# One joined state product in DeltaNet's scan, and HGRN2's recurrence over 128 tokens in place of two chunks of 64

## The chip, the cores and the metric

The kernel runs as one program on one core of a Trainium2 chip. The metric is the device time of one execution in microseconds (us). Engines: PE is TensorE, DVE is VectorE, ACT is ScalarE, POOL is GpSimd, SP is SyncE, which issues nearly all DMAs. A change of 0.3% is about what a measurement of this kernel can tell from no change.

## The reference

Two layers of a hybrid decoder trunk over 1024 tokens with a model width of 1024, all float32. Each layer normalises its input, projects it, feeds three groups of heads (A: sliding-window attention, B: HGRN2, C: gated DeltaNet), projects their joined output back, and ends with a SwiGLU feed-forward part of width 2816. What the change concerns are B and C, four heads of 64 each:

```python
# B, HGRN2: per chunk of 64 tokens and per head
kt = -expm1(lf); cum = cumsum(lf, axis=2)
attn = einsum('bhtd,bhsd,bhtsd->bhts', qt, kt, decay)   # decay = exp(cum_t - cum_s), s <= t
o = attn @ vt + einsum('bhtd,bhde->bhte', qt * exp(cum), state)
state = exp(last) * state + einsum('bhsd,bhse->bhde', kt * exp(last - cum), vt)
...
# C, gated DeltaNet: per chunk of 64 tokens and per head
v_new = u - w @ state
o = qd @ state + qkc @ v_new
state = gl * state + swapaxes(kd, -1, -2) @ v_new
...
out = rmsnorm(o, gain) * silu(gate)      # both groups
```

The result of B doesn't depend on the size of its chunks: a longer chunk holds more of the sum in `attn` and less in `state`.

## The kernel before, in words

The tokens are handled in two halves of 512, the layers in turn, so there are four passes (layer, half): (0,0), (0,1), (1,0), (1,1). In each, dense products (input projection, output projection, feed-forward) run on PE as three float32r products per block (lines 776 to 778 in `mm3`: high by high, and the two cross terms of a high/low split of both operands). Their weights come by DMA into `wraw`, ACT rounds them to `whi` (line 747), DVE makes the rest `wlo` (line 748).

The three head groups, the mixers, are Python generators: `gdn` (DeltaNet), `hgrn` and `attention`. Each handles four blocks of 128 tokens per pass, so 16 blocks in all. Every `yield` ends a step; the class `Pace` asks a `Weaver` for the next step after so many dense products (`tick`), so that the steps are strewn among the dense work of another stage: the mixers of (0,0) among input projections, those of the other three passes among the feed-forward part of the pass before. That fixes the order in which instructions are written down. Their order on each engine is then made by the tile framework's scheduler, which also hands out buffers: pools have a number of buffers per tag, and a tile whose pool is full waits until an earlier one was read for the last time. `k.pb` (3 PSUM banks) serves HGRN2 and attention, `k.pc` (2 banks) DeltaNet, `k.mp` (one buffer per tag) the SBUF tiles of the mixers.

A PE matrix product has a shape of array: operands of 64 rows and 64 columns use a 64x64 tile of the 128x128 array, and the profile writes `64*64`, `128*64` or `128*128` for it. A plain float32 product shows as two records in the trace, a transpose or a float32r product as one.

- `hgrn`, one block: lines 430 to 447 transpose `kk` (432), make the sums of log forget gates for six halving levels plus one in `pd` (four tiles of 448 columns, 438) and their exponentials `E`, and the decayed keys `kd` (444 to 447). Lines 450 to 457 multiply `E` with keys and queries into `X` for the levels 32, 16, 8, 4, 2, 1: keys on POOL for odd places in the list, on DVE for even, queries on DVE. Lines 459 to 477: 64x64 products per level into `pl` (470), which DVE picks together into `st` under masks (474, 477). Lines 479 to 502, twice, once per chunk of 64: output from the state (484, operands of 64 columns), from `st` (488), the state's update (494) and four DVE instructions on 64x64 that put it into `sB` (500). `finish` follows.
- `gdn`, one block: lines 574 to 608 load and normalise; 610 to 623 transpose keys, queries, decayed queries `qd` and `kb` and copy them out (`qdT` is used by the scan); 633 to 638 are the 64x64 products `pkk`, of which 643 and 644 on DVE make `AT` and `qkT` from the tiles r = 0 and r = 1; then a triangular solve on DVE (654 to 669). Lines 694 to 722, twice, once per chunk: `w` by the state (701, 64 columns), new values `vn` on DVE (703), then decayed queries by the state (706, 64 columns), `qkT` by `vn` (709) and the state's update (715), and four DVE instructions (720).
- `finish` (376 to 396) squares the output of one block on ACT (384), multiplies by the gate on DVE (385), scales by a reciprocal root, transposes (392), and stores to `mix`. Its tile `f_sq` has the tag `f1`, one buffer for HGRN2 and DeltaNet.
- `build_consts` makes the masks and sums on POOL and DVE at the start (lines 89 to 124).

Of the kernel before, what the change touches and what calls it, by code (L numbers as in the profile page):

```python
# [29 lines left out]
LEVELS = [32, 16, 8, 4, 2, 1]  # L30
LN_FLOOR = 60
# [31 lines left out]
def build_consts(k, positions):  # L63
# [5 lines left out]
    mc = t1[:, 0:896].rearrange("p (l t) -> p l t", l=7)  # L69
    idt = t1[:, 896:1024]  # L70
# [26 lines left out]
    sel(mc[:, 6, :], [[1, 128]], 0, -1)  # L97
    G.memset(mc[0:64, 6, 64:128], 0.0)
    k.mc = cp.tile([128, 7, 128], F32R, name="mcr")
    V.tensor_copy(k.mc, mc)  # L100
    k.tri = k.mc[:, 6, :].bitcast(F32)
# [18 lines left out]
    k.cst = cp.tile([128, 128], F32R, name="cst")  # L120
    G.memset(mk, 1.0)
    sel(mk, [[-1, 128]], -1, 1)
    G.memset(mk[64:128, 0:64], 0.0)
# [252 lines left out]
def finish(k, mixr, po, gate, t0, b, pt, junk):  # L376
    nc = k.nc
    V, A, G, T = nc.vector, nc.scalar, nc.gpsimd, nc.tensor
    sp = k.mp
    p4 = po.rearrange("p (h d) -> p h d", d=64)  # L380
    sq = sp.tile([128, 4, 64], F32, name="f_sq", tag="f1")
    ss = k.small.tile([128, 4], F32, name="f_ss")
    for j in range(4):
        A.activation(junk[:, j, :], p4[:, j, :], AF.Square, accum_out=ss[:, j:j + 1])
    V.tensor_tensor(out=sq, in0=p4, in1=gate.rearrange("p (h d) -> p h d", d=64), op=ALU.mult)
    r = k.small.tile([128, 4], F32, name="f_r")
    rsqrt(k, r, ss, 4, 1.0 / 64, EPS)
    V.tensor_tensor(out=sq, in0=sq, in1=bc(r[:, :, None], (128, 4, 64)), op=ALU.mult)
    yield 6.0
    pt = pt()  # L390
    for p in range(2):
        T.transpose(pt[:, p, :], sq[:, 2 * p:2 * p + 2, :].rearrange("p a b -> p (a b)"), k.ident)
    ot = sp.tile([128, 4, 128], F32, name="f_ot", tag="fo")
    A.activation(ot[:, 0:2, :], pt, AF.Copy)
    nc.sync.dma_start(out=mixr[:, t0:t0 + 2, 128 * b:128 * b + 128], in_=ot[:, 0:2, :])
    yield 0.0


def hgrn(k, lc, l, h, src, r2):
# [4 lines left out]
    E = r2[:, 0:1792].rearrange("p (a l t) -> p a l t", a=2, l=7)  # L404
    X = r2[:, 1792:3328].rearrange("p (a l t) -> p a l t", a=2, l=6)
    kT = r2[:, 3328:3584].rearrange("p (a t) -> p a t", a=2)
    qd = r2[:, 3584:3840].rearrange("p (a t) -> p a t", a=2)
    st = r2[:, 3840:4096].rearrange("p (r a t) -> p r a t", r=2, a=2)
# [12 lines left out]
    for b in range(NB):  # L421
        nc.sync.dma_start(out=ld[:, 512:1024], in_=tmr[:, b, C_BV:C_BV + 512])
        qT = mp.tile([128, 2, 128], F32, name="h_qT")
# [10 lines left out]
        for p in range(2):  # L434
            for hf in range(2):
                pd = k.pb.tile([128, 448], F32, name="pd", tag="b")
                for i, t_ in enumerate((lfh, lfl)):
                    T.matmul(pd, t_[:, 128 * p:128 * p + 128], mcf[:, 448 * hf:448 * hf + 448],
                             start=(i == 0), stop=(i == 1))
                A.activation(E[:, p].rearrange("p l t -> p (l t)")[:, 448 * hf:448 * hf + 448], pd, AF.Exp)  # L440
            yield 0.3
        pe = k.pb.tile([128, 256], F32, name="pe", tag="b")
        for i, t_ in enumerate((lfh, lfl)):
            T.matmul(pe, k.cst, t_, start=(i == 0), stop=(i == 1))
        kd = mp.tile([128, 256], F32, name="h_kd")
# [4 lines left out]
        for i, H in enumerate(LEVELS):  # L450
            ev = E[:, :, i, :].rearrange("p a (b s j) -> p a b s j", s=2, j=H)
            xv = X[:, :, i, :].rearrange("p a (b s j) -> p a b s j", s=2, j=H)
            for s_, t_, eng in ((0, kT, G if i % 2 else V), (1, qT, V)):
                tv = t_.rearrange("p a (b s j) -> p a b s j", s=2, j=H)
                eng.tensor_tensor(out=xv[:, :, :, s_, :], in0=tv[:, :, :, s_, :],
                                  in1=ev[:, :, :, s_, :], op=ALU.mult)
        V.tensor_tensor(out=qd, in0=qT, in1=E[:, :, 6, :], op=ALU.mult)
        yield 4.0
        for lv in ((0, 1, 2, 3), (4, 5, 6)):
            pl = [k.pb.tile([128, 4, 2, 64], F32, name=f"pl{r}", tag="b") for r in range(2)]  # L460
            for li, i in enumerate(lv):
                for p, r, c in ((0, 0, 0), (0, 1, 1), (0, 0, 1), (0, 1, 0),
# [3 lines left out]
                    if i < 6:  # L466
                        lh = rh = X[rows, p, i, cols]
# [11 lines left out]
        pou = k.pb.tile([128, 512], F32, name="hpo", tag="b")  # L479
        po = pou[:, 0:256]  # L480
        for c in range(2):
            cols = slice(64 * c, 64 * c + 64)
            for p in range(2):
                T.matmul(po[cols, 128 * p:128 * p + 128], qd[:, p, cols], k.sB[:, p, :],
                         start=True, stop=False)
                for r in range(2):
                    o = 128 * p + 64 * r
                    T.matmul(po[cols, o:o + 64], st[cols, r, p, :], vv[cols, o:o + 64],
                             start=False, stop=(r == 1))
            pu = pou[:, 256 + 128 * c:384 + 128 * c].rearrange("p (a d) -> p a d", a=2)  # L490
            for p in range(2):
                for r in range(2):
                    o = 128 * p + 64 * r
                    T.matmul(pu[64 * r:64 * r + 64, p, :], kd[cols, o:o + 64], vv[cols, o:o + 64],
                             start=True, stop=True)
            for p in range(2):
                for r in range(2):
                    rows = slice(64 * r, 64 * r + 64)
                    sv = k.sB[rows, p, 64 * r:64 * r + 64]
                    V.scalar_tensor_tensor(out=sv, in0=sv, scalar=E[rows, p, 6, 64 * c + 63:64 * c + 64],  # L500
                                           in1=pu[rows, p, :], op0=ALU.mult, op1=ALU.add)
            yield 1.2
        yield from finish(k, mixr, po, gate, 4, b,
                          lambda: k.pb.tile([128, 2, 128], F32, name="hf_pt", tag="b"),
                          qT.rearrange("p a (r d) -> p (a r) d", r=2))


def gdn(k, lc, h, src, r4):
# [9 lines left out]
    kt = r4[3][:, 0:768].rearrange("p (u a t) -> p u a t", u=3, a=2)  # L518
    L = r4[3][:, 768:1024].rearrange("p (h d) -> p h d", h=4)
# [52 lines left out]
    for b in range(NB):  # L572
        nc.sync.dma_start(out=gate, in_=tmr[:, b, C_CG:C_CG + 256])
# [25 lines left out]
        qd = mp.tile([128, 4, 64], F32, name="g_qd", tag="g1")  # L599
# [11 lines left out]
        p2 = k.pc.tile([128, 4, 128], F32, name="g_p2", tag="c")  # L611
# [8 lines left out]
        A.activation(kt[:, 2], p2[:, 0:2, :], AF.Copy)  # L620
        A.activation(kt[:, 0:2].rearrange("p a b t -> p (a b) t"), p1, AF.Copy)
        qdT = mp.tile([128, 2, 128], F32, name="g_qdT")
        A.activation(qdT, p2[:, 2:4, :], AF.Copy)
# [64 lines left out]
        pw = k.pc.tile([128, 2, 128], F32, name="g_pw", tag="c")  # L688
        for p in range(2):
            T.transpose(pw[:, p, :], fl(wu[:, 0, 2 * p:2 * p + 2, :]), k.ident)  # L690
        wT = mp.tile([128, 2, 128], F32, name="g_wT", tag="g1")
        A.activation(wT, pw, AF.Copy)
        yield 1.0
        pop = k.pc.tile([128, 512], F32, name="g_po", tag="c")
        po, ps_ = pop[:, 0:256], pop[:, 256:512]
        pu2 = k.pc.tile([128, 2, 2, 64], F32, name="g_pu", tag="c")
        vn = mp.tile([128, 4, 64], F32, name="g_vn", tag="g1b")
        for c in range(2):
            cols = slice(64 * c, 64 * c + 64)
            for p in range(2):  # L700
                T.matmul(ps_[cols, 128 * p:128 * p + 128], wT[:, p, cols], k.sC[:, p, :], start=True, stop=True)
            vv = fl(vn[cols])
            V.tensor_tensor(out=vv, in0=fl(wu[cols, 1]), in1=ps_[cols], op=ALU.subtract)
            yield 0.8
            for p in range(2):
                T.matmul(po[cols, 128 * p:128 * p + 128], qdT[:, p, cols], k.sC[:, p, :], start=True, stop=False)  # L706
                for r in range(2):
                    hh = 2 * p + r
                    T.matmul(po[cols, 64 * hh:64 * hh + 64], qkT[cols, r, p, :], vn[cols, hh, :],
                             start=False, stop=(r == 1))  # L710
            pu = pu2[:, c]
            for p in range(2):
                for r in range(2):
                    hh = 2 * p + r
                    T.matmul(pu[64 * r:64 * r + 64, p, :], kd[cols, hh, :], vn[cols, hh, :], start=True, stop=True)
            for p in range(2):
                for r in range(2):
# [3 lines left out]
                                           in1=pu[rows, p, :], op0=ALU.mult, op1=ALU.add)  # L721
# [816 lines left out]
```

## Time and profile before

| | |
|---|---|
| median of 3 runs | 2784.97 us (2778.39 to 2785.39) |
| the profiled execution | 2783.36 us, of which its span 2781.6 us |
| PE, matmuls | busy 2667.4 us, 96% of the span |
| DVE | 1868.2 us, 67% |
| ACT | 1127.4 us, 41% |
| POOL | 358.2 us, 13% |
| mean granted TensorE clock | 0.993 of full speed |

A time in the rows further on counts from the start of the span. A timeline row gives the start, the duration, the engine, the line, the operation, output and inputs, shapes, and the number of records merged into it; the duration of a PE record includes the way through the array, so what a product takes from PE is read from start to start.

### The profile page before, as it was taken

The numbers are of one execution on the slowest core, as the hardware profiler recorded it, in microseconds if no ns is written. First come the engines' busy times: TensorE is split into PE (matmuls) and PEld (weight loads), VectorE is DVE, ScalarE is ACT, GpSimd is POOL, SyncE is SP. The second block draws the span as 40 slices with busy tenths as digits, with TensorE's granted clock in tenths as the row PEclk, the third lists the DMA queues.
The fourth block names the chain that finished last, engine by engine and source line by source line (L and its number), as shares of the span: only waits on it lengthen the run. The fifth ranks groups of instructions, "written<-read, shape, count | busy, mean of one in ns | idle before, by whom it ended". The sixth has DMA issues, their size and how long they took to land. (4 is left out here: it accounts for less than half of the span.)

```text
span 2781.6 us, 43050 instructions
## 1 busy us (share of the span) xinstructions
PE 2667.4 (96%) x15744; PEld 2127.4 (76%) x15744; DVE 1868.2 (67%) x4877; ACT 1127.4 (41%) x2257; POOL 358.2 (13%) x540
## 2 busy tenths in 40 slices
PE   4999898999999999999999999999999999999999
PEld 3887766777777778887777777897777777788887
DVE  7679876777868567567886757637777845644444
ACT  4635653333444444433244444543334444322222
POOL 5121210301101001311011001211101100100000
PEclk9999999999999999999999999999999999999999
DMA  6643326542333355534333335452332224332323
GB/s 233 199 154 121 113 89 207 163 125 88 119 112 100 108 167 164 181 119 123 118 106 100 106 124 177 131 160 68 95 111 82 69 74 158 115 95 91 95 79 107
DMA packets 171699, 343.97 MB, mean 124 GB/s; under 512 B 20576, under 2 KB 80224, under 8 KB 171488
## 3 DMA queue, kind: packets, MB, share of 16 engines
q1 hardware_dynamic: 170624, 341.16, 38.9%
q8 instruction: 124, 2.03, 0.3%
q14 instruction: 87, 0.71, 0.1%
q10 hardware_dynamic: 864, 0.07, 0.0%
HBM read 299.15 MB, written 42.01 MB: 123 GB/s over the span
## 5 line engine op out<-in xcount | busy, mean ns | idle before, releaser
L747 ACT ACTIVATE whi<-wraw 128x1024 fp32r<-128x1024 f32 (+3 forms) x484 | 422.7, 874 | 820.0 <-PE dn_ps L777 228.0
L748 DVE TENSOR_TENSOR wlo<-wraw,whi 128x1024 fp32r<-128x1024 f32 (+3 forms) x484 | 493.7, 1021 | 264.0 <-ACT whi L747 255.2
L776 PE MATMUL gu_ps<-hhi,whi 128*128 128x512 f32 x1408 | 570.6, 405 | 4.1 <-DVE n_xn L825 3.3
L778 PE MATMUL gu_ps<-hhi,wlo 128*128 128x512 f32 x1408 | 559.2, 397 | 0.0
L777 PE MATMUL gu_ps<-hlo,whi 128*128 128x512 f32 x1408 | 557.9, 396 | 0.8 <-DVE hlo L829 0.8
L776 PEld LDWEIGHTS gu_ps<-hhi,whi 128*128 128x128 f32 x1408 | 266.4, 189 | 76.4 <-issue 15.9
L778 PEld LDWEIGHTS gu_ps<-hhi,wlo 128*128 128x128 f32 x1408 | 265.2, 188 | 61.4 <-issue 0.8
L777 PEld LDWEIGHTS gu_ps<-hlo,whi 128*128 128x128 f32 x1408 | 265.9, 189 | 58.1 <-DVE hlo L829 2.9
L776 PE MATMUL dn_ps<-gt,whi 128*128 128x512 f32 x704 | 288.7, 411 | 1.3 <-DVE xt L1038 1.1
L777 PE MATMUL dn_ps<-gt,whi 128*128 128x512 f32 x704 | 279.3, 397 | 1.5 <-DVE gt L1026 1.4
L778 PE MATMUL dn_ps<-gt,wlo 128*128 128x512 f32 x704 | 278.4, 395 | 0.0
L777 PE MATMUL p_tm<-wlo,hhi 128*128 128x256 f32 (+1 forms) x896 | 255.4, 285 | 7.2 <-DVE wlo L748 7.2
L776 PE MATMUL p_tm<-whi,hhi 128*128 128x256 f32 (+1 forms) x896 | 255.9, 286 | 4.5 <-ACT cx L852 2.5
L778 PE MATMUL p_tm<-whi,hlo 128*128 128x256 f32 (+1 forms) x896 | 254.8, 285 | 0.0
L777 PEld LDWEIGHTS p_tm<-wlo,hhi 128*128 128x128 f32 x896 | 170.0, 190 | 10.6 <-DVE wlo L748 9.3
L776 PEld LDWEIGHTS p_tm<-whi,hhi 128*128 128x128 f32 x896 | 170.0, 190 | 7.8 <-ACT cx L852 3.4
L778 PEld LDWEIGHTS p_tm<-whi,hlo 128*128 128x128 f32 x896 | 169.7, 189 | 2.2 <-issue 1.8
L776 PEld LDWEIGHTS dn_ps<-gt,whi 128*128 128x128 f32 x704 | 132.7, 189 | 39.5 <-issue 9.2
L777 PEld LDWEIGHTS dn_ps<-gt,whi 128*128 128x128 f32 x704 | 132.9, 189 | 32.8 <-DVE gt L1026 6.5
L778 PEld LDWEIGHTS dn_ps<-gt,wlo 128*128 128x128 f32 x704 | 132.7, 188 | 30.9
L1038 DVE SCALAR_TENSOR_TENSOR xt<-dn_ps,gth,xt 128x512 f32<-128x512 f32 x144 | 107.8, 749 | 70.8 <-PE dn_ps L778 70.3
L1023 DVE TENSOR_TENSOR g_t<-g_t,gu_ps 128x512 f32<-128x512 f32 x88 | 60.2, 684 | 121.3 <-PE gu_ps L778 121.2
(403 smaller groups left out, 4462.5 us busy)
## 6 DMA issues: line engine op xcount, KB each, us to landing
wraw<-in_w_gate_dram SPq DMA_DIRECT2D x88, 512.0 KB, 3.3
wraw<-in_w_up_dram SPq DMA_DIRECT2D x88, 512.0 KB, 3.3
wraw<-in_ada_w_dram SPq DMA_DIRECT2D x80, 512.0 KB, 3.7
wraw<-in_w_down_dram SPq DMA_DIRECT2D x128, 256.0 KB, 2.7
wraw<-in_w_in_t_dram SPq DMA_DIRECT2D x48, 512.0 KB, 4.1
wraw<-in_w_in_f_dram SPq DMA_DIRECT2D x32, 512.0 KB, 3.7
wraw<-in_w_out_dram SPq DMA_DIRECT2D x32, 512.0 KB, 4.1
wraw<-in_w_down_dram SPq DMA_DIRECT2D x64, 192.0 KB, 2.4
```

What stands on the lines that cost most here:

```text
L747: nc.scalar.activation(hi[:, 0:n], raw[:, 0:n], AF.Copy)
L748: nc.vector.tensor_tensor(out=lo[:, 0:n], in0=raw[:, 0:n], in1=hi[:, 0:n].bitcast(F32), op=ALU.subtract)
L776: T.matmul(out, lh, rh, start=first, stop=False)
L777: T.matmul(out, lh, rl, start=False, stop=False)
L778: T.matmul(out, ll, rh, start=False, stop=last)
L1023: V.tensor_tensor(out=t, in0=t, in1=pss[1], op=ALU.mult)
L1038: V.scalar_tensor_tensor(out=x, in0=ps, scalar=k.gth[l][:, m:m + 1], in1=x, op0=ALU.mult, op1=ALU.add)
```

## The change

HGRN2: the list of levels gets a first entry of 64 (`HALVES`), so that one block of 128 tokens is one chunk. `E` gets that level, the products with keys and queries are written back into `E` in place of `X`. Four 64x64 products (keys of the first 64 tokens by queries of the last 64) join those of the last three levels, ACT copies them to `sx`, and POOL copies the lower half of `st` beside them. The state is read once per block with all 128 tokens, and updated once. `Finish` replaces `finish`, in two methods, so that parts of a block can be worked off.

DeltaNet: `w` and decayed queries of a chunk stand side by side in `wq`, and one product by the state gives both; the output of a chunk then lies in the other half of the partitions, so the gate is loaded with its halves swapped in two DMAs, and the last copy swaps them back. The transposes of `qd` move from the first transposes to behind `pkk`, into a PSUM tile `g_p3` of their own. The state's update comes ahead of `qkT` by `vn`.

```diff
+HALVES = [64] + LEVELS
+NL = len(HALVES)
...
@@ build_consts: one level more, k.tri a tile of its own, k.cst2 new
-    for i, H in enumerate(LEVELS):
+    for i, H in enumerate(HALVES):
...
+class Finish:
...
+    def __init__(self, k, mixr, gate, t0, b, pt, junk, swapped=False):
...
+        self.sq = k.mp.tile([128, 4, 64], F32, name="f_sq", tag="f1")
...
+    def part(self, po, rows=slice(0, 128)):
...
+        for j in range(4):
+            nc.scalar.activation(self.junk[rows, j, :], p4[:, j, :], AF.Square, accum_out=self.ss[rows, j:j + 1])
+        nc.vector.tensor_tensor(out=self.sq[rows], in0=p4, in1=self.g4[rows], op=ALU.mult)
...
@@ hgrn
-                pd = k.pb.tile([128, 448], F32, name="pd", tag="b")
+                pd = k.pb.tile([128, 512], F32, name="pd", tag="b")
...
-        for i, H in enumerate(LEVELS):
+        for i, H in enumerate(HALVES):
             ev = E[:, :, i, :].rearrange("p a (b s j) -> p a b s j", s=2, j=H)
...
+            if lv[0] > 0:
+                for p in range(2):
+                    for r in range(2):
+                        rows = slice(64 * r, 64 * r + 64)
+                        T.matmul(pl[r][0:64, 3, p, :], E[rows, p, 0, 0:64], E[rows, p, 0, 64:128], start=True, stop=True)
+                for r in range(2):
+                    A.activation(sx[0:64, r], pl[r][0:64, 3], AF.Copy)
...
+        G.tensor_copy(sx[64:128], st[64:128])
+        po = k.pb.tile([128, 256], F32, name="hpo", tag="b")
+        pu = k.pb.tile([128, 2, 128], F32, name="hpu", tag="b")
+        for p in range(2):
+            T.matmul(pu[:, p, :], kd[:, 128 * p:128 * p + 128], vv[:, 128 * p:128 * p + 128], start=True, stop=True)
+        for p in range(2):
+            T.matmul(po[:, 128 * p:128 * p + 128], qd[:, p, :], k.sB[:, p, :], start=(p == 0), stop=False,
+                     skip_group_check=True)
...
+        yield 1.2
         for c in range(2):
...
             for p in range(2):
                 for r in range(2):
                     o = 128 * p + 64 * r
...
+                    kr = slice(0, 64 + 64 * c)
+                    T.matmul(po[64 * c:64 * c + 64, o:o + 64], (st, sx)[c][kr, r, p, :], vv[kr, o:o + 64],
+                             start=False, stop=True, skip_group_check=True)
+        yield 1.0
...
@@ gdn
-        for j in range(2):
-            T.transpose(p2[:, 2 + j, :], fl(qd[:, 2 * j:2 * j + 2, :]), k.ident)
...
+        p3 = k.pc.tile([128, 2, 2, 64], F32, name="g_p3", tag="c")
+        for j in range(2):
+            T.transpose(fl(p3[:, j]), fl(qd[:, 2 * j:2 * j + 2, :]), k.ident)
+        A.activation(wq[:, :, 1:3, :], p3, AF.Copy)
...
+            pop = k.pc.tile([128, 512], F32, name="g_po", tag="c")
+            pq = pop[:, 0:256]
+            pu = pop[:, 256:384].rearrange("p (a d) -> p a d", a=2)
             for p in range(2):
...
+                T.matmul(pq[:, 128 * p:128 * p + 128], fl(wq[:, p, 2 * c:2 * c + 2, :]), k.sC[:, p, :],
+                         start=(p == 0), stop=False, skip_group_check=True)
+            V.tensor_tensor(out=fl(vn[cols]), in0=fl(wu[cols, 1]), in1=pq[cols], op=ALU.subtract)
             yield 0.8
             for p in range(2):
                 for r in range(2):
                     hh = 2 * p + r
+                    T.matmul(pu[64 * r:64 * r + 64, p, :], kd[cols, hh, :], vn[cols, hh, :],
+                             start=False, stop=True, skip_group_check=True)
+            for p in range(2):
+                for r in range(2):
+                    hh = 2 * p + r
+                    T.matmul(pq[oth, 64 * hh:64 * hh + 64], qkT[cols, r, p, :], vn[cols, hh, :],
+                             start=False, stop=True, skip_group_check=True)
...
+            fin.part(pq[oth], oth)
             yield 1.0
```

## Rows read from the trace of the kernel before

**Rows 1.** Stretches: length, busy us of PE, PEld, DVE, ACT, POOL; clock, DMA share, GB/s.
```profile
230.00:420.00 190.00, 174.11 (x1526) 135.15 (x1525) 158.83 (x613) 110.91 (x299) 34.26 (x59) 0.98 0.35 109
...
1160.00:1640.00 480.00, 471.61 (x2953) 369.17 (x2953) 346.98 (x1020) 186.32 (x428) 50.06 (x78) 1.00 0.39 118
```

**Rows 2.** Timeline of PE, DeltaNet's value step and the dense products around it.
```profile
1481.37 0.40 PE L778 MATMUL gu_ps<-hhi,wlo 128*128 128x512 f32 x1
1481.69 0.43 PE L706 MATMUL g_po<-sC,g_qdT 128*64 128x128 f32 x2
1482.06 0.44 PE L709 MATMUL g_po<-g_vn,g_qkT 64*64 64x64 f32 x4
...
1483.07 0.40 PE L715 MATMUL g_pu<-g_vn,g_kd 64*64 64x64 f32 x7
...
1483.73 0.40 PE L777 MATMUL gu_ps<-hlo,whi 128*128 128x512 f32 x1
```

**Rows 3.** Timeline of PE, DeltaNet's product of w and the state (line 701 between).
```profile
1473.60 0.39 PE L778 MATMUL dn_ps<-gt,wlo 128*128 128x512 f32 x1
...
1474.84 0.39 PE L777 MATMUL dn_ps<-gt,whi 128*128 128x512 f32 x1
```

**Rows 4.** Timeline of PE, one chunk of HGRN2's recurrence (lines 484, 488, 494 between).
```profile
1326.85 0.39 PE L777 MATMUL gu_ps<-hlo,whi 128*128 128x512 f32 x1
1327.08 0.39 PE L778 MATMUL gu_ps<-hhi,wlo 128*128 128x512 f32 x1
...
1329.43 0.40 PE L777 MATMUL gu_ps<-hlo,whi 128*128 128x512 f32 x1
```

**Rows 5.** Timeline of PE, eight float32 records on the whole array.
```profile
685.20 0.39 PE L778 MATMUL dn_ps<-gt,wlo 128*128 128x512 f32 x1
685.43 1.05 PE L684 MATMUL g_px<-g_RR,scr 128*128 128x128 f32 x8
...
686.55 0.39 PE L777 MATMUL dn_ps<-gt,whi 128*128 128x512 f32 x1
```

**Rows 6.** Timeline of PE, four levels of HGRN2, 64 records in 64x64 tiles.
```profile
1211.17 0.40 PE L778 MATMUL gu_ps<-hhi,wlo 128*128 128x512 f32 x1
1211.50 1.16 PE L470 MATMUL pl<-scr 64*64 64x64 f32 x64
...
1212.93 0.39 PE L777 MATMUL gu_ps<-hlo,whi 128*128 128x512 f32 x1
```

**Rows 7.** Groups by line, DVE and ACT: count, busy us, mean ns, idle before.
```profile
L500 DVE SCALAR_TENSOR_TENSOR sB<-sB,scr,hpo 64x64 f32<-64x64 f32 x128 | 35.9, 280 | 28.1 <-PE hpo L494 25.3
...
L455 DVE TENSOR_TENSOR scr<-h_qT,scr 128x128 f32<-128x128 f32 x96 | 31.3, 348 | 0.0
...
L384 ACT ACTIVATE g_wu<-g_po 128x64 f32<-128x64 f32 x64 | 13.4, 223 | 28.1 <-PE g_po L709 25.6 <-DVE wlo L748 2.6
```

**Rows 8.** Timeline of PE and DVE: next PE product after pkk, DVE's first qkT.
```profile
137.67 0.39 PE L777 MATMUL p_tm<-wlo,hhi 128*128 128x256 f32 x1
...
139.79 0.28 DVE L644 TENSOR_TENSOR g_qkT<-pkk,g_Li 128x128 f32<-128x128 f32 x1
...
1422.83 0.50 PE L776 MATMUL gu_ps<-hhi,whi 128*128 128x512 f32 x1
...
1427.66 0.28 DVE L644 TENSOR_TENSOR g_qkT<-pkk,g_Li 128x128 f32<-128x128 f32 x1
...
2198.96 0.50 PE L776 MATMUL gu_ps<-hhi,whi 128*128 128x512 f32 x1
...
2200.41 0.28 DVE L644 TENSOR_TENSOR g_qkT<-pkk,g_Li 128x128 f32<-128x128 f32 x1
```

**Rows 9.** Timeline of POOL and DVE in the first 40 us.
```profile
2.36 9.82 POOL L86 TENSOR_SCALAR_AFFINE_SELECT h_ld<-h_ld 128x64 f32<-128x64 f32 x25
...
34.49 0.27 DVE L114 CAST lmask<-cv 128x64 uint8<-128x64 f32 x1
...
36.80 0.68 DVE L1128 TENSOR_TENSOR hlo<-n_xn,hhi 128x512 fp32r<-128x512 f32 x1
```

More of the change, by code (lines that the diff above doesn't have):

```diff
@@ L373, in attention, with rest @@
         yield 0.0
[L376 to L396, printed above, removed]
+class Finish:
+    def __init__(self, k, mixr, gate, t0, b, pt, junk, swapped=False):
+        self.k, self.mixr, self.t0, self.b, self.pt, self.junk, self.swapped = k, mixr, t0, b, pt, junk, swapped
+        self.g4 = gate.rearrange("p (h d) -> p h d", d=64)
+        self.sq = k.mp.tile([128, 4, 64], F32, name="f_sq", tag="f1")
+        self.ss = k.small.tile([128, 4], F32, name="f_ss")
+    def part(self, po, rows=slice(0, 128)):
+        nc = self.k.nc
+        p4 = po.rearrange("p (h d) -> p h d", d=64)
+        for j in range(4):
+            nc.scalar.activation(self.junk[rows, j, :], p4[:, j, :], AF.Square, accum_out=self.ss[rows, j:j + 1])
+        nc.vector.tensor_tensor(out=self.sq[rows], in0=p4, in1=self.g4[rows], op=ALU.mult)
+    def rest(self):
+        k = self.k
+        nc = k.nc
+        r = k.small.tile([128, 4], F32, name="f_r")
+        rsqrt(k, r, self.ss, 4, 1.0 / 64, EPS)
+        nc.vector.tensor_tensor(out=self.sq, in0=self.sq, in1=bc(r[:, :, None], (128, 4, 64)), op=ALU.mult)
+        yield 6.0
+        pt = self.pt()
+        for p in range(2):
+            nc.tensor.transpose(pt[:, p, :], self.sq[:, 2 * p:2 * p + 2, :].rearrange("p a b -> p (a b)"), k.ident)
+        ot = k.mp.tile([128, 4, 128], F32, name="f_ot", tag="fo")
+        if self.swapped:
+            for c in range(2):
+                nc.scalar.activation(ot[:, 0:2, 64 * c:64 * c + 64], pt[:, :, 64 - 64 * c:128 - 64 * c], AF.Copy)
+        else:
+            nc.scalar.activation(ot[:, 0:2, :], pt, AF.Copy)
+        nc.sync.dma_start(out=self.mixr[:, self.t0:self.t0 + 2, 128 * self.b:128 * self.b + 128], in_=ot[:, 0:2, :])
+        yield 0.0
@@ L443, in hgrn @@
         for i, t_ in enumerate((lfh, lfl)):
[L444 to L445 removed]
+            T.matmul(pe, k.cst2, t_, start=(i == 0), stop=(i == 1))
         A.activation(kd, pe, AF.Exp)
@@ L478, in hgrn @@
             yield 2.0
-        pou = k.pb.tile([128, 512], F32, name="hpo", tag="b")
-        po = pou[:, 0:256]
-        for c in range(2):
[L482 to L490, printed above, removed]
+        G.tensor_copy(sx[64:128], st[64:128])
[6 more added lines that the diff above has]
+                     skip_group_check=True)
+        for p in range(2):
+            for r in range(2):
+                rows = slice(64 * r, 64 * r + 64)
+                sv = k.sB[rows, p, 64 * r:64 * r + 64]
+                V.scalar_tensor_tensor(out=sv, in0=sv, scalar=E[rows, p, NL, 127:128],
+                                       in1=pu[rows, p, 64 * r:64 * r + 64], op0=ALU.mult, op1=ALU.add)
+        yield 1.2
+        for c in range(2):
             for p in range(2):
@@ L493, in hgrn @@
                     o = 128 * p + 64 * r
[L494 to L505, printed above, removed]
+                    kr = slice(0, 64 + 64 * c)
+                    T.matmul(po[64 * c:64 * c + 64, o:o + 64], (st, sx)[c][kr, r, p, :], vv[kr, o:o + 64],
+                             start=False, stop=True, skip_group_check=True)
+        yield 1.0
+        fin = Finish(k, mixr, gate, 4, b, lambda: k.pb.tile([128, 2, 128], F32, name="hf_pt", tag="b"),
+                     qT.rearrange("p a (r d) -> p (a r) d", r=2))
+        fin.part(po)
+        yield from fin.rest()
 def gdn(k, lc, h, src, r4):
@@ L572, in gdn @@
     for b in range(NB):
-        nc.sync.dma_start(out=gate, in_=tmr[:, b, C_CG:C_CG + 256])
+        for c in range(2):
+            nc.sync.dma_start(out=gate[64 - 64 * c:128 - 64 * c, :], in_=tmr[64 * c:64 * c + 64, b, C_CG:C_CG + 256])
         pa = k.pc.tile([128, 2, 4, 64], F32, name="pa", tag="c")
@@ L721, in gdn @@
                                            in1=pu[rows, p, :], op0=ALU.mult, op1=ALU.add)
+            fin.part(pq[oth], oth)
             yield 1.0
-        yield from finish(k, mixr, po, gate, 6, b,
-                          lambda: k.pc.tile([128, 2, 128], F32, name="gf_pt", tag="c"), wu[:, 0])
+        yield from fin.rest()
 class Dense:
```

70 lines of the change are left out of this document (29 added, 41 removed).

## The prediction, made before the changed kernel had run

> **What bounds the kernel now.** I read the page's busy shares first, then the busy time by stretch, then the timeline of PE around single mixer steps. In a later pass PE's matmuls cover 471.6 of 480 us while DVE has 347.0 us of work; in the mixers of the first pass PE covers 174.1 of 190 us and DVE 158.8 [rows 1]. So over most of the span PE is the bound, and time is gained by whatever PE need no longer do; DVE is near to being a second bound in the first pass alone. The mixer steps stand between dense products, and there the price of one is read off directly: from the start of the last dense product before it to the start of the second one behind it, less two ordinary steps of 0.23 us, the distance of two dense products [rows 4]. The second one is taken because the first one after a step in small tiles is itself held up.
>
> **What a step costs, in three kinds.** Eight float32 records of 128 columns on the whole array: 686.55 - 685.20 - 0.46 = 0.89 us, 0.111 us a record, with nothing lost on entry or exit [rows 5]. 64 records of 64 columns in 64x64 tiles, four tiles in turn: 1212.93 - 1211.17 - 0.46 = 1.30 us; their starts fill 1.16 - 0.22 = 0.94 us, 0.0147 a record or 0.0585 for a round of four, and 0.365 us is left for entering and leaving the small tiles [rows 6] (0.22 is the way of one record through the array). Records that all use one tile come one per 0.0585 us. Where the tiles share their rows and alternate between two columns, as in line 715, seven start within 0.40 - 0.22 = 0.18 us [rows 2], so they run in pairs, 0.03 each. A change between 128-row and 64-row tiles inside a step: from the first record of line 706 to the first of line 709 are 0.37 us, of which two records take 0.22; 0.15 is the change [rows 2].
>
> The pairs are weighed against a rule. The Trainium skill, TensorEngine Tiling (Array Packing), Theoretical Speedup, gives products small in both directions up to four times their speed from 64x64 tiles. By that rule, the eight records of DeltaNet's update and the eight of the new level would take 0.12 us each time instead of the 0.24 and 0.23 used below, and the gain would be 48 x 0.12 = 6 us larger. The row shows four at a time only where the tiles change in both rows and columns, and pairs for this shape, so I keep the pairs.
>
> **The change, part by part**, per block of 128 tokens, 16 blocks:
> - DeltaNet's state product. Before, w alone with 64 columns: 1474.84 - 1473.60 - 0.46 = 0.78 us a chunk [rows 3]. After, w and queries together are four whole-array records, 4 x 0.111 = 0.445. Two chunks: -0.67.
> - DeltaNet's value step. Before 1483.73 - 1481.37 - 0.46 = 1.90 us a chunk [rows 2]. After, no product of queries and no change of tile within: 0.365 + 8 x 0.03 (update) + 8 x 0.0585 (qkT, one tile) = 1.07. Two chunks: -1.66.
> - HGRN2's recurrence. Before 1329.43 - 1327.08 - 0.46 = 1.89 us a chunk, 3.78 a block [rows 4]. After: update and state product are eight whole-array records, 0.89 [rows 5]; the products of st and sx are eight records in one 64x64 tile and eight in a 128x64 one, 0.365 + 16 x 0.0585 + 0.15 = 1.45. Together 2.34: -1.44.
> - The level of 64: eight records more, tiles alternating between two rows, 0.23; no entry, they follow others. The eight float32r products of `pd` grow by 64 columns, an eighth of a 0.23 us step each, together 0.23 [rows 4]. +0.46.
> - The transposes of qd: two whole-array records go from one step and come in another, 0.22 each way: 0.
>
> Sum -3.31 us a block, -53 us for 16.
>
> **What lies beside PE.** DVE gets two level products more (one for queries, one for keys, as POOL's share of the keys stays three), 0.35 each, and one gate product more per DeltaNet block, by its 256 columns one to two times a level product of 128; it loses four updates of 0.28 [rows 7]: between -0.1 and +0.3 us a block, nothing. ACT gets eight squares instead of four in DeltaNet and two copies to sx, POOL one copy. A square is 0.22 us [rows 7], as much again for the reading of its sum, so ACT gets at most 2.6 us a block; it is busy 58% of the first pass's stretch and 39% later [rows 1], PE's dense products cover it, and uncovered it would be those 2.6 us. SP gets one issue more per DeltaNet block, the second half of the gate, behind which weight loads queue; the weights are loaded several units ahead, so nothing. HGRN2's last products now wait for POOL's copy, which waits for the last mask on DVE: a step of 1.2 us lies between, and the dense products of that step cover it. `f_sq` is taken by DeltaNet before its first chunk and held to its transposes; HGRN2 needs the same buffer, so its finish, and the next load of its gate on SP, may be held back meanwhile. No dense product needs either until the pass's mix is split. In `build_consts` POOL gets four more masks of 9.82/25 = 0.39 us, and DVE three short copies: at most 2 us at the start, I take 1 [rows 9].
>
> **The one new wait on PE.** `g_p3` needs a bank of `k.pc`; both are then held by the two `pkk` tiles, so the transposes wait until DVE has made AT and qkT of r = 0, and if they stand right behind `pkk` in PE's queue, every dense product behind them waits too. The time from the next product after `pkk` to the end of that qkT is 140.07 - 137.67 = 2.40 us in the first block, 2200.69 - 2198.96 = 1.73 in the last, 5.11 in the worst (1427.94 - 1422.83); over the 16 blocks it comes to 35 us [rows 8]. That is the upper bound; the lower is nothing, since a wait can't give time. Which end is nearer hangs on the order on PE. The engines don't follow the written order: masks from `build_consts`, whose rest is written behind the whole of `first_pieces`, are cast at 34.49 us, ahead of that function's `hlo` at 36.80 [rows 9]. So the scheduler should put dense products ahead of transposes whose bank it counts as taken, and what is left is its error about DVE. I take a quarter of a microsecond a block, 4 us.
>
> **The sum.** -53, of which the four blocks of the first pass make 13; there DVE is as busy as it is, and I count half, +6.6. With 4 for the wait and 1 at the start: -41. Against the profiled execution, 2783.4 us (span 2781.6, and 1.8 around it; 1.6 below the median), that is 2742.
>
> **Rivals.**
> 1. The transposes do stand behind `pkk`, and the whole 35 us of [rows 8] are paid: -53 + 6.6 + 35 + 1 = -10, 2773. For it: they are written there, with no step between. Against: the order in [rows 9]. Chance 0.13.
> 2. DVE holds the mixers back, so that PE's shorter steps turn into waits: nothing gained in the first pass, half in the other three (40 us): -20, 2763. For it: DVE's 84% in the first pass. Against: 72% later [rows 1]. Chance 0.10.
> 3. Slower. The wait at `g_p3` costs not the mean of [rows 8] but its worst, since the dense products' DVE work, above all `wlo`, collects while PE stands: 16 x 5.1 = 82 us, -53 + 6.6 + 82 + 1 = +37, 2820. It decides from a mean wait of 2.8 us a block on, where the 45 us of gain are used up. For it: such a queue on DVE stands in the worst block. Against: a standing PE gives DVE time to catch up. Chance 0.05.
> 4. The change doesn't do what it says: the scheduler splits the joined steps, each piece paying its own 0.365, and little is left: 2780. Chance 0.02.
>
> **How the numbers follow.** The forecast has 0.70, with a range of its own from 2729 (all 53 us) to 2756 (its waits twice or thrice what I take). Rival 2 lies at -0.7%, rival 1 at -0.37%, so on the edge; 0.3% (8 us) is about what a measurement can tell from no change. Faster: 0.70 + 0.10 + half of rival 1 = 0.86. Same: the other half and rival 4, 0.08. Slower: 0.06. The range of 8 in 10 runs from 2729 to 2768: beyond it lie rivals 1, 3 and 4 and little else.
>
> **What would show it.** In the changed profile: DeltaNet's state product as four whole-array records between dense products, at about 0.45 us; its value step near 1.07, HGRN2's two steps near 0.89 and 1.45; PE's waits in a later pass no more than before; dense products between the last `pkk` and the first transposes of `g_p3`, and no wait of some microseconds in front of these. Wrong it would be if PE waited for line 644's successor 16 times over, or if the steps came out right and idle time on PE grew by as much.

## The result, and the profile after

The changed kernel takes 2743.68 us (median of 4 runs, 2739.38 to 2744.44) against 2782.94 us before: a ratio of 0.9858, 95% interval 0.984 to 0.9875. The profiled execution took 2744.08 us, 1.7 of it outside the span. Forecast were 2742 us with a range from 2729 to 2768.

The head of the page: the span, then busy us, share of the span and instructions of each engine.

```profile
span 2742.4 us, 42796 instructions
...
PE 2616.8 (95%) x15488; PEld 2117.0 (77%) x15488; DVE 1869.8 (68%) x4863; ACT 1158.3 (42%) x2434; POOL 377.9 (14%) x560
```

PE lost 2667.4 - 2616.8 = 50.6 us of work and the span 39.2, so some 11 us came back as idle time of PE. DVE's work is what it was (1868.2 before).

The same stretches as in [rows 1], by the view of busy time per stretch (length, busy us of PE, PEld, DVE, ACT, POOL; clock, DMA share, GB/s):

```profile
230.00:420.00 190.00, 168.58 (x1510) 136.01 (x1510) 167.42 (x622) 122.10 (x349) 36.84 (x63) 0.97 0.39 121
1160.00:1640.00 480.00, 470.12 (x2891) 373.20 (x2891) 351.14 (x1030) 196.44 (x477) 52.99 (x81) 1.00 0.39 119
```

The later pass is bound by PE as before. In the mixers of the first pass DVE and PE are now equally busy, 167 and 169 of 190 us: the same DVE work in a shorter time.

**The steps on PE.** The timeline of PE around each new step, with the last dense product before it and, behind it, the second one (DeltaNet's state product; HGRN2's update and state product; DeltaNet's value step; HGRN2's products of `st` and `sx`; the last three levels, line 484, with the new one, line 489). They stand in order of time:

```profile
1253.34 0.39 PE L801 MATMUL dn_ps<-gt,wlo 128*128 128x512 f32 x1
1253.57 0.60 PE L725 MATMUL g_po<-sC,scr 128*128 128x128 f32 x4
...
1254.24 0.39 PE L800 MATMUL dn_ps<-gt,whi 128*128 128x512 f32 x1
...
1255.87 0.39 PE L801 MATMUL dn_ps<-gt,wlo 128*128 128x512 f32 x1
1256.19 0.93 PE L484 MATMUL pl<-scr 64*64 64x64 f32 x48
1256.94 0.41 PE L489 MATMUL pl<-scr 64*64 64x64 f32 x8
...
1257.62 0.39 PE L800 MATMUL dn_ps<-gt,whi 128*128 128x512 f32 x1
...
1259.26 0.40 PE L801 MATMUL dn_ps<-gt,wlo 128*128 128x512 f32 x1
1259.49 0.61 PE L504 MATMUL hpu<-h_ld,scr 128*128 128x128 f32 x4
1259.93 0.61 PE L506 MATMUL hpo<-sB,scr 128*128 128x128 f32 x4
...
1260.62 0.39 PE L800 MATMUL dn_ps<-gt,whi 128*128 128x512 f32 x1
...
1262.23 0.39 PE L801 MATMUL dn_ps<-gt,wlo 128*128 128x512 f32 x1
1262.55 0.45 PE L732 MATMUL g_po<-g_vn,g_kd 64*64 64x64 f32 x8
1262.84 0.63 PE L737 MATMUL g_po<-g_vn,g_qkT 64*64 64x64 f32 x8
...
1263.74 0.39 PE L800 MATMUL dn_ps<-gt,whi 128*128 128x512 f32 x1
...
1264.67 0.39 PE L801 MATMUL dn_ps<-gt,wlo 128*128 128x512 f32 x1
1264.98 1.28 PE L520 MATMUL hpo<-h_ld,scr 64*64 64x64 f32 x16
...
1266.54 0.40 PE L800 MATMUL dn_ps<-gt,whi 128*128 128x512 f32 x1
```

From the start of the dense product before to the second one behind, less 0.46, as in the prediction: state product 0.90 - 0.46 = 0.44 us, recurrence 0.90, value step 1.05, products of `st` and `sx` 1.41, levels 1.29. In the later passes the same steps take nearly the same time wherever they stand between dense products without a wait.

**The new wait.** The first rows of the view of PE's waits (us in total, times, longest):

```profile
PE n_ps L831 <- POOL cv L88: 19.2, 1, 19.2
PE g_p L666 <- DVE g_qkT L663: 17.3, 10, 3.5
...
PE pt L358 <- ACT scr L354: 6.2, 2, 5.8
PE g_px L696 <- DVE scg L692: 6.0, 4, 5.1
```

PE stands 17.3 us in front of the transposes of `qd` (line 666), 10 times; no such row was there before. The wait for attention's `pt`, on the other hand, was more than twice as long before:

```profile
PE pt L353 <- ACT scr L349: 13.9, 8, 5.9
```

In the passes (1,0) and (1,1) the waits in front of the transposes, 4.4 and 3.2 us, stand where 2.4 and 1.9 us of waits for `pt` are gone. So part of the new wait takes the place of an old one. The longest of the new ones, in the timeline of PE and DVE:

```profile
1400.64 0.67 PE L657 MATMUL pkk<-scr 64*64 64x128 f32 x16
...
1401.19 1.22 DVE L1175 SCALAR_TENSOR_TENSOR wraw<-wraw,cond 128x1024 f32<-128x1024 f32 x1
1401.24 0.50 PE L799 MATMUL gu_ps<-hhi,whi 128*128 128x512 f32 x1
...
1402.04 0.40 PE L799 MATMUL gu_ps<-hhi,whi 128*128 128x512 f32 x1
...
1403.59 1.22 DVE L771 TENSOR_TENSOR wlo<-wraw,whi 128x1024 fp32r<-128x1024 f32 x1
...
1405.52 0.28 DVE L663 TENSOR_TENSOR g_qkT<-pkk,g_Li 128x128 f32<-128x128 f32 x1
...
1405.95 0.41 PE L666 MATMUL g_p<-identr,g_qd 128*128 128x128 f32 x2 [3.51 <-DVE g_qkT L663]
1406.12 0.47 PE L800 MATMUL gu_ps<-hlo,whi 128*128 128x512 f32 x1
```

Four dense products stand between `pkk` and the transposes. They last until 1402.44; the `qkT` that frees the bank ends at 1405.80, since two long products on weights (lines 1175 and 771) and others stand ahead of it on DVE. Meanwhile the next dense product waits behind the transposes.

**Where the time went**, by the starts of the first and last products into `gu_ps` of each feed-forward part, in the profiled executions before and after: the first pass comes to its feed-forward part 7.1 us earlier, the mixers of (0,1), (1,0) and (1,1), strewn among the feed-forward parts, take 6.3, 12.8 and 13.0 us off, and all other stages together nothing. These figures come from one execution of each kernel; between executions of the same kernel those of the first two passes differ by up to 3.6 us (7.1, 5.6 and 7.2 for the first pass of the changed kernel, 6.3, 9.9 and 7.3 for (0,1)), those of the other two by less than 1.

### The profile page after: what moved, and what is told of

Same layout as the page of the kernel before. It is cut to its first block, busy times and chain, and to the rows that moved or that the text cites. A ratio compares the mean times of both kernels' runs of the same rounds, so it can differ in the third digit from the quotient of the medians.

```text
span 2742.4 us, 42796 instructions
## 1 busy us (share of the span) xinstructions
PE 2616.8 (95%) x15488; PEld 2117.0 (77%) x15488; DVE 1869.8 (68%) x4863; ACT 1158.3 (42%) x2434; POOL 377.9 (14%) x560
## 4 chain that ended last, share of the span: by engine, by line
PE 67%; DVE 17%; issue 5%; POOL 4%; ACT 4%; DMA 2%; SPq 0%; POOLq 0%; ACTq 0%; DVEq 0%
PE gu_ps L799 10%; PE gu_ps L800 9%; PE gu_ps L801 9%; PE dn_ps L799 5%; PE dn_ps L800 5%; PE dn_ps L801 5%; DVE wlo L771 3%; PE p_tm L800 2%; PE p_tm L801 2%; PE p_tm L799 2%; PE o_ps L800 2%; PE o_ps L801 2%; PE o_ps L799 2%; POOL n_xn L850 1%; PE pl L484 1%
## 5 line engine op out<-in xcount | busy, mean ns | idle before, releaser
L799 PEld LDWEIGHTS gu_ps<-hhi,whi 128*128 128x128 f32 x1408 | 267.4, 190 | 74.0 <-issue 13.9
```

Source lines behind the costliest of these rows:

```text
L799: T.matmul(out, lh, rh, start=first, stop=False)
```

## The experiments

Kernels tried together share runs of the kernel before on the same chip (e1 to e4: 2780.35 us; e5 to e8: 2779.16; e9 to e11: 2780.9), and ratios and gains are against these. Line numbers of the changed kernel are used throughout.

**e1: qd's transposes later**, behind the triangular solve, when both `pkk` tiles have long been read.

```diff
-        p3 = k.pc.tile([128, 2, 2, 64], F32, name="g_p3", tag="c")
-        for j in range(2):
-            T.transpose(fl(p3[:, j]), fl(qd[:, 2 * j:2 * j + 2, :]), k.ident)
-        A.activation(wq[:, :, 1:3, :], p3, AF.Copy)
...
             V.transpose(TT[rows, :, 32 * q:32 * q + 32].rearrange("p m (i w) -> p i m w", w=8), fl(U[rows]))
+        p3 = k.pc.tile([128, 2, 2, 64], F32, name="g_p3", tag="c")
+        for j in range(2):
+            T.transpose(fl(p3[:, j]), fl(qd[:, 2 * j:2 * j + 2, :]), k.ident)
+        A.activation(wq[:, :, 1:3, :], p3, AF.Copy)
```

> Only the two transposes of qd, their bank g_p3 and the copy to wq are moved, from behind pkk to behind the triangular solve. Theory: the 17.3 us that TensorE waited before them in the changed kernel (10 waits on DVE's first qkT) were paid in full, so they go: 2743.7 - 17 = about 2726 us, and the profile shows no wait of these transposes above 2 us in all. Rival: the wait stood in for others (DVE's queue, the dense products' wlo) that are now late in its place: no gain, 2740 to 2745 us.

2734.91 us, ratio 0.9839 (0.9824 to 0.9855), 8.8 us below the first runs of the changed kernel: faster than the rival's bound, and half of the gain that was expected. The wait in front of the transposes falls from 17.3 to 1.6 us, but only half of that reaches the time. PE's wait for attention's `pt` grows meanwhile from 6.2 us, nearly back to the 13.9 that it was before the change:

```profile
PE pt L358 <- ACT scr L354: 12.0, 6, 6.0
```

**e2: DeltaNet's part alone** (`gdn` and `Finish` of the changed kernel; `hgrn`, its masks and its `finish` as before). Against the changed kernel:

```diff
-HALVES = [64] + LEVELS
...
-            T.matmul(po[:, 128 * p:128 * p + 128], qd[:, p, :], k.sB[:, p, :], start=(p == 0), stop=False,
...
+                T.matmul(po[cols, 128 * p:128 * p + 128], qd[:, p, cols], k.sB[:, p, :],
...
+                    T.matmul(pu[64 * r:64 * r + 64, p, :], kd[cols, o:o + 64], vv[cols, o:o + 64],
```

> The kernel before with DeltaNet's part of the change alone. Theory: two chunks of 0.31 + 0.86 us less per block, 37 us over 16 blocks, less the 17 us of the wait at g_p3: 20 us below the kernel before, 2763 us. Rival: most of the gain is HGRN2's, and DeltaNet's is eaten by the wait: within 6 us of the kernel before, 2777 to 2783 us.

2770.86 us, ratio 0.9964 (0.9951 to 0.9978): -9.5 us, half of what was expected and more than the rival allowed, with 17.5 us of wait at `g_p3`. By the starts of the stages, as above, its three later passes took 3.2, 4.5 and 6.7 us off; the steps make 9.3 us a pass, and the waits at `g_p3` in them are 5.7, 4.4 and 3.2, which leaves 3.6, 4.9 and 6.1. So the later passes came as the theory has them, and the shortfall lies in the first pass, which came to its feed-forward part 4.0 us later than before.

**e3: HGRN2's part alone** (`gdn` and its `finish` as before). Against the changed kernel:

```diff
-        p3 = k.pc.tile([128, 2, 2, 64], F32, name="g_p3", tag="c")
...
-                T.matmul(pq[:, 128 * p:128 * p + 128], fl(wq[:, p, 2 * c:2 * c + 2, :]), k.sC[:, p, :],
...
+                T.matmul(ps_[cols, 128 * p:128 * p + 128], wT[:, p, cols], k.sC[:, p, :], start=True, stop=True)
...
+                T.matmul(po[cols, 128 * p:128 * p + 128], qdT[:, p, cols], k.sC[:, p, :], start=True, stop=False)
```

> The changed kernel with DeltaNet as it was before: HGRN2's part alone, with its masks at the start. Theory: 1.48 us less in the recurrence and 0.46 more for the new level and the wider pd, 1.0 us a block, 16 us, less 2 us at the start: 14 us below the kernel before, 2769 us. Rival: the recurrence of 128 tokens also takes away waits of TensorE on DVE's state update, and gives more than its instructions, 25 us: 2758 us.

2766.3 us, ratio 0.9949 (0.9932 to 0.9966): -14 us, as the theory has it. Added up, the two parts make -23.5, and together they gave -39.

**e4: the state product unjoined**, everything else as changed.

```diff
-                T.matmul(pq[:, 128 * p:128 * p + 128], fl(wq[:, p, 2 * c:2 * c + 2, :]), k.sC[:, p, :],
+                for q in range(2):
+                    T.matmul(pq[64 * q:64 * q + 64, 128 * p:128 * p + 128], wq[:, p, 2 * c + q, :], k.sC[:, p, :],
                          start=(p == 0), stop=False, skip_group_check=True)
```

> The changed kernel with w and the decayed queries multiplied by the state in two products of 64 columns each in place of one of 128, all else as changed. Theory: what joining saves is the entry into and exit from smaller tiles, 0.33 us a chunk, since products that alternate between two columns run in pairs: +11 us on the changed kernel, 2754 us. Rival 1: they run one after another, so 0.45 us more a chunk come on top: +25 us, 2769 us. Rival 2: what counted was the order of the value step alone, and joining is worth nothing: 2744 us.

2752.42 us, ratio 0.9904 (0.9885 to 0.9923), 8.7 us above the changed kernel, near the 11 of the forecast by pairs. The step in the timeline of PE, where line 726 has taken the place of 725, and then the product of w alone in the kernel before:

```profile
1251.47 0.39 PE L802 MATMUL dn_ps<-gt,wlo 128*128 128x512 f32 x1
1251.79 0.66 PE L726 MATMUL g_po<-sC,scr 128*64 128x128 f32 x8
...
1252.72 0.39 PE L801 MATMUL dn_ps<-gt,whi 128*128 128x512 f32 x1
```

```profile
1473.92 0.65 PE L701 MATMUL g_po<-sC,g_wT 128*64 128x128 f32 x4
```

1.25 - 0.46 = 0.79 us in place of 0.44. That is the price that w alone had before, 0.78 [rows 3], and eight records take the 0.66 us that four took: the queries' records run beside those of w in the other 64 columns and come free, and what the join saves is the change of tiles, since on the whole array all of it costs 0.44.

**e5: e2 with the transposes later**, with the same diff as e1, in e2.

> DeltaNet's part alone, as in e2, but with the transposes of qd behind the triangular solve, as in e1. The terms of the prediction for this part, -0.67 and -1.66 us a block, make -37 us, with the first pass counted half -33. Theory 1: what e2 fell short of that (it gave -9.5) is the wait at g_p3 with all that follows from it, in the first pass above all: 33 us below the kernel before, ratio 0.988. Theory 2: the wait is worth here what e1 showed it to be worth in the full change, 9 us: 18 us below, ratio 0.9935, and the rest of e2's shortfall has another cause. Below 0.9905 it is theory 1, above 0.992 theory 2.

2757.76 us, ratio 0.9921 (0.9897 to 0.9945): -21.4 us, 12 better than e2. The ratio lies on theory 2's side of its bound, but the interval takes in both bounds (-29 to -15 us), so it doesn't decide. The runs of this one kernel lie between 2753.42 and 2763.37, and they fall in the order of their clocks (below).

**e6: a buffer of its own for DeltaNet's `f_sq`**, that of `AT`.

```diff
-        self.sq = k.mp.tile([128, 4, 64], F32, name="f_sq", tag="f1")
+        self.sq = k.mp.tile([128, 4, 64], F32, name="f_sq", tag="g1" if swapped else "f1")
```

> The change with f_sq of DeltaNet's finish in the buffer of AT, which is dead by then, so that HGRN2's finish never waits for DeltaNet's. Theory (of the prediction): the time from HGRN2's last product to its f_sq falls from 16 us in 7 blocks to below 6 us everywhere, and the time stays within 3 us of the changed kernel, as no dense product needs either. Rival: a late finish holds back the next load of HGRN2's gate and with it steps of the first pass: 5 us or more below the changed kernel.

From HGRN2's last product to its `f_sq` pass 15.5 to 18.6 us in 7 of 16 blocks of the changed kernel, 5.3 at most before, and 5.4 at most in e6. The time is 2746.19 us, ratio 0.9877 (0.9857 to 0.9897), against 2742.09 for the changed kernel on the same chip. That is 4 us more, one beyond the theory's 3, but the intervals of the two ratios overlap: no gain, so the finish is held back and no cost of it shows.

**e7 and e10: qd transposed early**, in the second half of `p2` as before the change, into a `wq` that lies in the place of `nrm`; `g_p3` is gone. e10 is the same kernel a second time.

```diff
-    wq = r4[3][:, 0:512].rearrange("p (a c t) -> p a c t", a=2, c=4)
+    wq = r4[2][:, 0:512].rearrange("p (a c t) -> p a c t", a=2, c=4)
...
+            T.transpose(p2[:, 2 + j, :], fl(qd[:, 2 * j:2 * j + 2, :]), k.ident)
...
+        A.activation(wq[:, :, 1:3, :], p2[:, 2:4, :].rearrange("p a (c t) -> p a c t", c=2), AF.Copy)
```

> The change with qd transposed beside qn and kb in the step of p1 and p2, in p2's second half, and the joined operand wq in the place of nrm (dead by then) in place of that of kt: g_p3, its bank and its wait are gone, and two records of 0.11 us stand in a step that is there anyway. Theory: all the wait of 17 us goes and nothing else takes its place: 13 to 17 us below the changed kernel, 2727 to 2731 us. Rival 1: as in e1, half of it comes back as waits of the next steps (pt for ACT): 9 us below, 2735 us, same as e1 within 3 us. Rival 2: the copy of qd into nrm's place makes the next block's nrm wait for the state products, and it is slower than e1 by over 5 us.

> The kernel of e7 (qd transposed beside qn and kb, no g_p3), beside the changed kernel on the same chip. At the same clock its spans lay 2 us below the changed kernel's. Theory: 2 to 4 us below the changed kernel, as e9 within 2 us, since both take the wait at g_p3 away and both get part of it back as waits of attention's pt for ACT. Rival: over 6 us below.

2739.04 us, ratio 0.9859 (0.9836 to 0.9881), and 2741.16, ratio 0.9863 (0.9847 to 0.988): 3 and 2 us below the changed kernel run beside them. Neither the 13 to 17 us of e7's theory came nor the 9 of its rival 1, though what rival 1 says of the waits did; 2 us is what e10's theory has, but it lay 3.4 us from e9, not within 2. The wait at `g_p3` is gone altogether, and the one for attention's softmax is again what it was before the change, 13.9 us, or a little more (e7):

```profile
PE pt L358 <- ACT scr L354: 15.1, 8, 7.4
```

**e8, e9, e11: the changed kernel and e1's kernel again**, e8 beside e7, e9 and e11 beside e10.

> The changed kernel itself, unaltered, on the same chip as e5 to e7: 2743 us, ratio 0.986, within 0.2% of its first runs.

> The kernel of e1 (qd's transposes behind the triangular solve), beside the changed kernel on the same chip. Over the 9 runs of the changed kernel and the 4 of e1 so far, the spans lie 6 us apart, of which the granted clock (0.9900 and 0.9915 in the mean) explains nearly half, as the spans of one kernel fall by 1.9 us for each 0.001 of it. Theory: the place of the transposes is worth 3 us at the same clock: 2736 us, ratio 0.9835 to 0.985. Rival: it is worth the 9 us of the first comparison: 2733 us or less, ratio below 0.983. Rival 2: nothing: ratio of the changed kernel's within 0.0005.

> The changed kernel itself on the same chip as e9 and e10: 2741 us, ratio 0.986 within 0.001; runs with a mean granted clock of 0.992 below 2740, runs with 0.988 above 2742.

The changed kernel: 2742.09 us, ratio 0.986 (0.9835 to 0.9885), and 2743.49, ratio 0.9866 (0.9851 to 0.988). e9: 2737.73 us, ratio 0.9845 (0.9831 to 0.986), 5.8 us below it, so between the 3 of the theory and the 9 of the rival; its ratio is the theory's. In e9 the transposes cost 0.22 to 0.23 us in 11 of the 15 blocks where they stand alone between dense products, and the wait is gone but for two or three. This kernel has the lowest medians of all that ran, 2735 and 2738 us against 2742 to 2744 for the changed one and 2739 and 2741 for e7's; between it and e7's kernel the intervals overlap. What was expected of e11 by the clock couldn't be seen: its runs had 0.989 to 0.991, and in so narrow a range the clock doesn't order them.

**The clock.** Every run lists its span and its mean granted clock, the share of full speed that TensorE was allowed. Within one kernel, the spans fall by 1.8 us for each 0.001 of the clock (74 runs of nine kernels, each against its own mean), and with that taken out the variance of what is left is halved (standard deviation 3.0 us without, 2.0 with it). This is a relation between runs; it doesn't say which is the cause. Brought to a clock of 0.991 by that slope:

| kernel | runs | mean span | mean clock | span at 0.991 | to before |
|---|---|---|---|---|---|
| before | 24 | 2778.5 | 0.9919 | 2780.2 | |
| changed (and e8, e11) | 13 | 2740.7 | 0.9899 | 2738.8 | -41 |
| e1, e9: qd later | 8 | 2735.1 | 0.9910 | 2735.1 | -45 |
| e7, e10: qd early | 8 | 2739.6 | 0.9892 | 2736.5 | -44 |
| e2: DeltaNet alone | 5 | 2768.8 | 0.9862 | 2760.2 | -20 |
| e5: DeltaNet alone, qd later | 4 | 2756.3 | 0.9895 | 2753.7 | -26.5 |
| e3: HGRN2 alone | 4 | 2764.8 | 0.9922 | 2767.0 | -13 |
| e4: unjoined | 4 | 2752.2 | 0.9885 | 2747.7 | -32.5 |
| e6: own f_sq | 4 | 2744.1 | 0.9882 | 2739.2 | -41 |

The clock isn't a condition from outside here: it differs from kernel to kernel, and the last section shows it falling where PE stands. So the last two columns tell how much of a difference goes along with the clock, not what a kernel would take without it. e2 has the lowest clock of all; -20 in its row is the figure that was expected, but the expectation was of the time, and there it was missed. The gap between the parts and the whole is 10 us by the measured times (e5 and e3 -35.5, e1 -45.5) and some 5 us at the same clock (-39.5 and -45), with about 3.5 of uncertainty. By the starts of the stages its largest part lies in the first pass, where e5 and e3 together gave 2.3 us, e1 10.2 and e9 7.5. Why it is there is open.

## Why the prediction was right, and where it was not

**The steps of PE held.** State product 0.44 (0.445 forecast), value step 1.05 (1.07), recurrence 0.90 + 1.41 = 2.31 (2.34). The new level behind the last three: eight records in 0.41 us, of which 0.22 are the way through the array, as the pairs have it. The work of PE fell by 50.6 us where 53 were summed. That the products of DeltaNet's update run in pairs is plain in line 732: eight records in 0.45 us, 0.23 for seven starts, where the eight records of line 737, all in one tile, need 0.63 - 0.22 = 0.41. The rule weighed in the prediction (the Trainium skill, TensorEngine Tiling (Array Packing), Theoretical Speedup) gives up to twice the speed for each direction of at most 64. From it the prediction took four at a time, 0.12 us, as the other possibility, and the measurement decides for the pairs. It is no case against the rule, though: the eight records of the update, and those of the new level, lie in two of the four tiles only, so they can't show what four would do. One tile takes a record every 0.0585 us, two in turn take one every 0.03, and the four of [rows 6] one every 0.0147, so the rows agree with a gain that grows with the number of tiles in use. All 24 state products of the later passes stand unsplit between dense products, at 0.44 to 0.45 us, which answers rival 4.

**The wait at `g_p3` was mis-sized as standing time.** The step that failed is "what is left is its error about DVE. I take a quarter of a microsecond a block, 4 us." The order was as argued, dense products ahead of the transposes, but in 14 of the 16 blocks these are three to five, which cover 0.8 to 1.4 us, and DVE's queue was often longer, up to 4.5 us from the last `pkk` to the first `qkT`: 17.3 us of standing, 1.1 a block in place of a quarter and half of the upper bound of 35. The sign named in the prediction, no wait of some microseconds in front of the transposes, failed with it. On the time the wait costs less: 9 us in the first comparison, 5.8 in the last, 5.6 between the mean spans of all 21 runs, 3.7 at the same clock (2738.8 - 2735.1, with about 1.8 of uncertainty); the last figure leaves out what the wait may cost by way of the clock. The rest was no loss against the kernel before: the wait for attention's `pt` had been 13.9 us, it fell to 6.2 in the changed kernel and rose to 12.0 without the wait at `g_p3`. So the 4 of the sum was near the price by luck: I took the wait to be short, and it is long and stands partly in the place of another. Rival 1, the transposes right behind `pkk` and 35 us paid, is refuted by the order and by the time, and rival 3 by the time. That even the 17.3 us are paid whole, which e1 set out to show, e1, e7 and e9 refute.

**Half for the first pass came in size, but not by the reason given.** It gave 7.1 us (5.6 and 7.2 in e8 and e11), where the sum has 13.25 / 2 less 1 at the start, 5.6. The half was argued from DVE: PE's shorter steps would turn into waits. DVE is as busy there as PE in the stretch shown above. But over the whole pass, from the first product into `p_tm` to the first into `gu_ps`, PE stands hardly longer than it did (before, changed, e2, e5; columns of [rows 1]):

```profile
73.49:519.52 446.03, 406.01 (x3113) 338.07 (x3113) 347.11 (x1076) 226.45 (x489) 83.56 (x121) 0.98 0.46 148
75.52:512.44 436.92, 397.55 (x3050) 338.90 (x3049) 349.98 (x1072) 235.38 (x534) 86.94 (x125) 0.97 0.48 150
72.72:523.51 450.79, 408.74 (x3081) 345.83 (x3081) 351.01 (x1080) 232.24 (x526) 84.23 (x121) 0.95 0.46 147
72.66:519.87 447.21, 406.19 (x3081) 343.11 (x3081) 350.70 (x1080) 232.75 (x526) 85.20 (x121) 0.95 0.46 148
```

Length less busy time is 40.0, 39.4, 42.1 and 41.0 us. What grew is PE's work at the lower clock, 0.50 in the profile: 12.6, 17.7, 34.9 and 29.6 us of its busy time, and there the same records take about twice as long (last section). By an estimate from these figures, half of the growth is lost: 2.5, 11.1 and 8.5 us, against 13.25 us of steps in the changed kernel and 9.3 in e2 and e5. That is most of what DeltaNet's part alone fell short by in this stretch (11.1 of 14.1 us in e2, 8.5 of 10.5 in e5), 2.5 of 4.1 us in this execution of the changed kernel, and by the same estimate all of it in e8 and e11 (7.8 of 7.5, 5.0 of 4.4). What made the clock lower there is open. Rival 2, steps that turn into waits, is thus not what the first pass shows, and it is wrong for the later passes, where 12.8 and 13.0 of 13.25 us came, and 13.7 and 13.6 in e1. The pass (0,1) gave 6.3 of 13.25 (9.9 in e8, 7.3 in e11), and 11.4 and 12.3 with the transposes later (e1, e9): what was missing there is the wait at `g_p3` for the most part, not the steps.

**The start** took 2.0 us more up to the first product into `p_tm` in the profiled execution (1 forecast, 2 the bound), of which POOL's masks are seen in the timeline of POOL:

```profile
2.46 12.08 POOL L88 TENSOR_SCALAR_AFFINE_SELECT h_ld<-h_ld 128x64 f32<-128x64 f32 x29
```

12.08 - 9.82 = 2.26 us [rows 9]. In the ten profiled executions with HGRN2's new masks that product starts at 73.6 to 75.5 us, 74.6 in the mean; in the three without them (before, e2, e5) at 72.7 to 73.5, 73.0 in the mean. So about 1.7 us go with the masks.

**ACT, SP and `f_sq`** cost nothing that a run showed. ACT has 1158.3 - 1127.4 = 30.9 us more work over the run, 1.9 us a block (2.6 at most forecast). e6 shows it for `f_sq`; for ACT and SP no run tested it alone.

## What to carry to other kernels

Where small steps stand strewn among dense products, read the price of a step from start to start of the dense products around it: four such prices came out within 0.04 us, and their sum gave the work that left PE within 5%. A wait in PE's queue should be sized by the queue of the engine that ends it, here by DVE's long weight products, not by the mean gap. When it is taken away, a fifth to a half of the standing time is gained here, since part of it stood in the place of another wait; so compare it with the waits of the kernel before. A transpose into a scarce PSUM bank is better put where the bank's last reader is long done (e1), or into a bank that it shares (e7); which of the two is better the runs don't show.

## What the runs showed of the hardware that was not expected

The time hangs on the granted clock more than I had expected. The busy time of one stretch of the changed kernel's first pass, in the columns of [rows 1], and three groups of eight whole-array float32 records in PE's timeline, the third behind that stretch:

```profile
284.00:294.20 10.20, 5.48 (x20) 4.89 (x21) 8.11 (x27) 5.17 (x15) 1.60 (x3) 0.50 0.29 96
```

```profile
288.04 2.08 PE L696 MATMUL g_px<-g_RR,scg 128*128 128x128 f32 x8 [5.10 <-DVE scg L692]
290.80 2.07 PE L702 MATMUL g_pz<-g_x,scg 128*128 128x128 f32 x8 [0.69 <-ACT g_x L698]
...
294.50 1.05 PE L707 MATMUL g_px<-g_RR,scg 128*128 128x128 f32 x8
```

Through 10.2 us the grant is 0.50, the lower of the two levels (1.2 GHz), and the same eight records take 2.08 us in place of 1.05. When it fell, PE had stood for a microsecond, waiting for DVE's triangular solve (5.10 us in all). If it is the wait that lowers the grant, such a wait is paid twice, once standing and once at half speed. Each of the eleven falls in this execution before its last microseconds came while PE stood or soon after; five of them came at waits in front of the transposes of `qd`, and five other waits there were followed by none. That is an order in time, not a cause shown. In the changed kernel 41 of the 55 us at this level lie in the first 560 us of the span, where PE waits for other engines; in e2 55 of 75 us. The mean clock of a kernel's runs ranges from 0.9862 (e2) to 0.9922 (e3), which by 1.8 us for 0.001 makes 11 us of time, more than most of these experiments had to tell apart. Where e2 has its low clock is shown, why it has it is not: no run filled PE's waits to raise it.
